# Two transformer blocks on one core: second products of the first weight pair by k, latents' weights in other slots, gate rows and convolutions beside the values

## The chip, the cores and the metric

The kernel runs on 1 core of one Trainium2 chip. A core has a tensor engine (TensorE, PE; PEld is its weight load), a vector engine (VectorE, DVE), a scalar engine (ScalarE, ACT), GpSimd (POOL), the queue engine that issues nearly all DMAs here (SyncE, SP), and 16 DMA engines. Each engine works through its own row of instructions in order and waits on semaphores for the others. The metric is device time in microseconds, median over runs.

## The reference

Two blocks follow one another on 1024 tokens of width 1024, in fp32. The change touches a matrix product of the first block's FFN and the input projection of the second block:

```python
def swiglu(h, w_in, w_out):
    a, b = jnp.split(h @ w_in, 2, axis=-1)
    return (jax.nn.silu(a) * b) @ w_out

# mixer_sublayer of the second block
proj = h @ w_in
(q_m, k_m, v_m, o_m, i_m, f_m, c_q, c_kv, k_r, gate_pre) = jnp.split(proj, IN_SPLIT_POINTS, axis=-1)
qk = jax.nn.silu(causal_depthwise_conv(jnp.concatenate([q_m, k_m], axis=-1), conv_w, conv_b))
log_i = (i_m + igate_b).astype(jnp.float32)
log_f = jax.nn.log_sigmoid((f_m + fgate_b).astype(jnp.float32))
y_m = mlstm_chunkwise(q_m, k_m, v_m, log_i, log_f).reshape(B, S, M_V_WIDTH)
q_a = rms_norm(c_q, q_norm_g) @ w_uq
```

`mlstm_chunkwise` is a recurrence over chunks: inside a chunk a masked product of queries and keys is weighted by exponentials of running sums of `log_f` and `log_i`. The second block then has attention on latents, a merge and a mixture of 32 experts, which the change leaves alone.

## The kernel before

**Products.** Every fp32 operand is cut into a high part (ACT copies it, L163) and a low part (DVE subtracts, L164), and a product is three matmuls: high x high, high x low, low x high (`mm3`, L219 to L221). Weights come by DMA into a `raw` tile and are split into a pair of tiles: `wh`/`wl` from a ring in the weight pool, `uh`/`ul` from the ring `k4`, or a place in a big region (here named `PU`, `SP` or `ML` by what it holds; it is one memory that is reused).

**Order.** A scheduler orders each engine's row from priorities that follow the order in which the code emits; a pool hands out a slot when its last user is done.

**`seven`.** A Strassen-like scheme computes two weight tiles (a pair) times the activations in seven products. It is called twice: in the first block's FFN and in the projection of the second block. The activations of the other half of the tokens come as four sums t1 to t4 and the part "11", made in four steps of k by `block_sums`: 16 PE transposes (L609), four ACT steps (L621, L629 and splits) and nine DVE steps each. The first weight pair is done in the usual way, so that PE has work: `usual_first` for the first half of the tokens, and `usual_second`, called after `block_sums` has ended, for the second half: per weight tile a PSUM tile and 24 matmuls, then an add (L772). Behind them the first Strassen pair starts (L672 on `SP`, whose operands DVE makes by L646 to L653 and splits).

**Projection of the second block**, after `seven(12)`: first the *latents*, eight token tiles of 356 columns (320 for `c_kv` and `k_r`, 36 for the gates, L1006 to L1026), with weights in region `PU`. Per tile ACT reads the PSUM tile, DVE computes a norm in some ten small steps (L105 to L124), ACT writes `ck`, `kr` and `gates` (L1016 to L1020), DVE rotates (L1051 to L1054), PE transposes the gates (L1024) and ACT writes them into the rows LI and FG (L1025, L1026). Then the code emits the eight convolutions (`conv`: a load, four DVE steps L961 and L964, a SiLU on ACT, a store). Then the *values*: two halves `nh` of the columns, eight token tiles each, 24 matmuls of 512 columns per tile; ACT evicts (L1042), SP stores (L1043). The second half's weights lie in `PU`.

**Mixer.** `block2_mixer` begins with `gate_rows` (L1063 to L1100): a chain of DVE and ACT steps on rows of 4 x 1024, which stores two rows to DRAM (`rr`) and transposes LI and FG on PE (L1097, L1098). `mlstm` then runs chunk by chunk between other products (`cq`, L1193): it loads `qkd`, `rr` and `vd` (L1121, L1122, L1127) into the region, now `ML`; POOL makes the decay matrix `Dm` (L1130), ACT its exponentials (L1132), PE the scores (L1135), DVE multiplies (L1137).

Of the kernel before, what the change touches and what calls it, by code (L numbers as in the profile page):

```python
# [11 lines left out]
F32R = mybir.dt.float32r  # L12
I32 = mybir.dt.int32
AF = mybir.ActivationFunctionType
# [6 lines left out]
NT = 8  # L21
# [14 lines left out]
class Kernel:  # L36
# [639 lines left out]
    def seven(self, n, src, B, norms, done, after, beside, kept=None):  # L676
# [4 lines left out]
        nc, V = self.nc, self.nc.vector  # L681
        TH, TL = self.TH, self.TL
        W, TT = {}, {}
# [14 lines left out]
        def first_two(j):  # L698

            A, T = self.left_parts(W[j]), self.T  # L700
            TT[j] = t = {}
            ps = self.pany()
            self.product(ps, A["a11"], T["00"])
            t[0] = self.h2([128, 512], "p1")
            nc.scalar.activation(t[0], ps, AF.Copy)
            yield
            ps = self.pany()
            self.product(ps, A["a12"], T["10"])
            t[2] = self.h2([128, 512], "c11")
            V.tensor_tensor(t[2], ps, t[0], op=OP.add)  # L710
            done(j, 0, 0, t[2], None)
# [37 lines left out]
        parts = [self.left_parts(C[0:2]), self.left_parts(C[2:4])]  # L749
        p1 = []  # L750
# [14 lines left out]
                yield  # L765

        def usual_second():
            for n, (A, p) in enumerate(zip(parts, p1)):
                ps = self.pany()
                self.mm3(ps, [(A[x][0][k], A[x][1][k], self.T[y][0][k], self.T[y][1][k])  # L770
                              for x, y in (("a11", "t1"), ("a12", "11")) for k in range(4)])
                V.tensor_tensor(p, ps, p, op=OP.add)  # L772
                done(0, n, 1, p, p1[0])

        f = usual_first()
        for _ in norms:
            next(f, None)
        for _ in f:
            pass
        f = first_two(1)  # L780
        for _ in self.block_sums(B, kept):
            next(f, None)
        usual_second()
        SP = self.region(1, "SP", F32R)
        for _ in prep(1, True):
            pass
# [182 lines left out]
    def block2_proj(self):  # L969
        nc, tc, a = self.nc, self.tc, self.a  # L970
        dram, const = self.dram, self.const
        W = "w_in_2"
        self.cqd = dram.tile([S, 704], F32, name="cqd")
        self.vd = dram.tile([S, D], F32, name="vd")
        self.gd = dram.tile([16, 128, S], F32, name="gd")
        self.ymd = dram.tile([S, D], F32, name="ymd")

        self.qkr, self.qkd, self.og = [dram.tile([8, 128, S], F32, name=n) for n in ("qkr", "qkd", "og")]
        x01d = dram.tile([4, 128, 512], F32, name="x01d")
        tiles = [(m * 128, self.qkr[m]) for m in range(8)] + [(2048 + m * 128, self.og[m]) for m in range(8)]  # L980
        tiles += [(3784 + m * 128, self.gd[m]) for m in range(8, 16)]

        def done(j, c, half, t, first):
            nc.sync.dma_start(tiles[2 * j + c][1][:, half * 512:half * 512 + 512], t)

        self.seven(12, lambda j: [self.wcols(W, c0, 128) for c0, _ in tiles[2 * j:2 * j + 2]], self.B3, self.norms2, done,
                   lambda: None, lambda j, n: None, x01d)
        for k in range(4):
            t = self.h2([128, 512], "x01")
            nc.sync.dma_start(t, x01d[k])  # L990
            self.split(self.TH[:, k, 512:1024], self.TL[:, k, 512:1024], t)

        cs = self.k4([128, 2, NT, 64], "cs")
        nc.sync.dma_start(cs[:, 0], a["rope_cos"].rearrange("(i p) c -> p i c", p=128))
        nc.sync.dma_start(cs[:, 1], a["rope_sin"].rearrange("(i p) c -> p i c", p=128))
        gb = const.tile([36, 1], F32, name="gbias")
        nc.sync.dma_start(gb[0:4, :], a["igate_b_2"].rearrange("o h -> h o"))
        nc.sync.dma_start(gb[32:36, :], a["fgate_b_2"].rearrange("o h -> h o"))
        self.LI, self.FG = self.k4([4, S], "LI"), self.k4([4, S], "FG")
        PU = self.region(1, "PU", F32R)  # L1000
        units = []
        for u in range(4):
            raw = self.wp.tile([128, 1024], F32, name="raw", bufs=self.raw_bufs)[:, 0:712].rearrange("p (k c) -> p k c", k=2)
            nc.gpsimd.memset(raw[:, :, 324:352], 0.0)
            for c0, n, at in ((3464, 320, 0), (3072, 4, 320), (3076, 4, 352)):
                nc.sync.dma_start(raw[:, :, at:at + n],  # L1006
                                  a[W][0, u * 256:u * 256 + 256, c0:c0 + n].rearrange("(k p) m -> p k m", p=128))
            h, l = [PU[:, 2 * u + n, 0:712].rearrange("p (k c) -> p k c", k=2) for n in range(2)]
            self.split(h, l, raw)
            units += [(h[:, j], l[:, j]) for j in range(2)]  # L1010
        for i in range(NT):
            ps = self.pany((128, 356))
            self.token_rows(ps, i, units)
            ck = self.h2([128, 320], "ck")
            r = self.rstd(self.sumsq(ps[:, 0:256], ck[:, 0:256]), 1, 1.0 / 256)
            nc.scalar.activation(ck[:, 0:256], ps[:, 0:256], AF.Copy, scale=r)  # L1016
            kr = self.h2([128, 2, 64], "kr")
            nc.scalar.activation(kr[:, 0], ps[:, 256:320], AF.Copy)
            gt = self.k2([128, 36], "gates")
            nc.scalar.activation(gt, ps[:, 320:356], AF.Copy)  # L1020
            self.rope(ck[:, 256:320], kr[:, 0], kr[:, 1], cs, i, 1)
            nc.sync.dma_start(self.cqd[i * 128:(i + 1) * 128, 384:704], ck)
            pt, s = self.ptp((36, 128)), slice(i * 128, i * 128 + 128)
            nc.tensor.transpose(pt, gt, self.ident)  # L1024
            nc.scalar.activation(self.LI[:, s], pt[0:4], AF.Identity, bias=gb[0:4])  # L1025
            nc.scalar.activation(self.FG[:, s], pt[32:36], AF.Identity, bias=gb[32:36])  # L1026
        for m in range(8):
            self.conv(m)

        self.yd = dram.tile([S, D], F32, name="yd")  # L1030
        z = self.k4([128, D], "zero")
        nc.gpsimd.memset(z, 0.0)
        for i in range(NT):
            nc.sync.dma_start(self.yd[i * 128:(i + 1) * 128, :], z)

        for nh in range(2):
            units = self.kunits(W, 1024 + nh * 512, 512, 2, 3, PU if nh else None)
            for i in range(NT):
                ps = self.pany()
                self.token_rows(ps, i, units)  # L1040
                t = self.k2([128, 512], "vt")
                nc.scalar.activation(t, ps, AF.Copy)  # L1042
                nc.sync.dma_start(self.vd[i * 128:(i + 1) * 128, nh * 512:nh * 512 + 512], t)  # L1043
# [130 lines left out]

    def block2_mixer(self, dbg=None):
        nc, tc, a = self.nc, self.tc, self.a
        self.gate_rows()
        step = self.mlstm()

        units = []  # L1180
# [822 lines left out]
```

## Time and profile before

| | |
|---|---|
| runs | 2828.6, 2821.66, 2820.65 us; median 2821.66 |
| profiled execution | 2824.64 us |
| its span | 2822.9 us, 36499 instructions |
| mean granted TensorE clock | 0.968 of 2.4 GHz |
| busy share | PE 93%, PEld 75%, DVE 67%, ACT 45%, POOL 8% |

The span runs from the first to the last instruction of the profiled execution; its time is 1.7 us more. Times in the views are microseconds from the span's start. A line in brackets behind a row, as "[6.69 <-DVE SD L1137]", says how long the engine was idle before it and what ended that.

### The profile page before, as it was taken

What the parts mean: (1) busy time and instruction counts of PE and PEld (TensorE: products, weight loads), DVE (VectorE), ACT (ScalarE), POOL (GpSimd) and SP (SyncE); (2) the same over time, 40 slices, a digit from 0 to 9 for tenths busy, and PEclk for the clock granted to TensorE, in tenths of its full rate; (3) what the DMA queues carried; (4) which work ended last, traced back from release to release, by engine and by line L of the source; (5) the groups of instructions that cost most, each with busy time, mean ns of one, the idle gap of its engine ahead of it and who ended that gap; (6) DMA issues with size and microseconds to landing.
All of it is one profiled execution on the core that took longest, in us unless ns stands there. A gap on an engine that the chain in (4) does not pass through costs nothing. (4 is left out here: it accounts for less than half of the span.)

```text
span 2822.9 us, 36499 instructions
## 1 busy us (share of the span) xinstructions
PE 2615.4 (93%) x13018; PEld 2107.2 (75%) x13018; DVE 1884.3 (67%) x3826; ACT 1283.1 (45%) x2258; POOL 221.2 (8%) x207
## 2 busy tenths in 40 slices
PE   6999998999999999889998999999999999889992
PEld 4766676788888787678886788788887887777771
DVE  5666549988887332886558264647778478788885
ACT  4666645333333210342125254425556434677772
POOL 0000002000000000200000000000000200443320
PEclk8999999999999999999999999999999999899996
DMA  7333123455555952533356465650111454799995
GB/s 244 90 98 98 37 75 120 128 165 163 178 172 167 290 181 92 170 106 113 104 159 222 134 184 174 197 194 21 31 31 53 158 196 157 248 335 329 312 319 179
DMA packets 329806, 453.14 MB, mean 161 GB/s; under 512 B 42401, under 2 KB 223710, under 8 KB 329622
## 3 DMA queue, kind: packets, MB, share of 16 engines
q1 hardware_dynamic: 320406, 433.98, 46.8%
q0 software_dynamic: 9216, 16.81, 2.5%
q8 instruction: 103, 1.69, 0.2%
q14 instruction: 81, 0.66, 0.1%
HBM read 360.16 MB, written 107.31 MB: 166 GB/s over the span
## 5 line engine op out<-in xcount | busy, mean ns | idle before, releaser
L163 ACT ACTIVATE wh<-raw 128x1024 fp32r<-128x1024 f32 (+1 forms) x101 | 104.6, 1039 | 185.6 <-DMA raw<-in_ffn_w_in_dram 44.5
L164 DVE TENSOR_TENSOR wl<-raw,wh 128x1024 fp32r<-128x1024 f32 (+1 forms) x101 | 126.0, 1250 | 69.3 <-ACT wh L163 67.1
L551 POOL TENSOR_TENSOR Y<-Y,G 128x1024 f32<-128x1024 f32 x16 | 39.5, 2466 | 1157.1 <-ACT junk L159 1151.9
L164 DVE TENSOR_TENSOR mgl<-X,MH 128x1024 fp32r<-128x1024 f32 x91 | 110.0, 1220 | 12.8 <-ACT MH L163 12.1
L1805 PEld LDWEIGHTS pss<-mgl,xh 128*128 128x128 f32 x512 | 96.9, 189 | 22.6
L252 DVE SCALAR_TENSOR_TENSOR acc<-raw,cc,acc 128x1024 f32<-128x1024 f32 x70 | 89.8, 1282 | 33.9 <-DMA raw<-in_mod_w_dram 31.2
L163 ACT ACTIVATE MH<-X 128x1024 fp32r<-128x1024 f32 x91 | 96.3, 1061 | 32.8 <-DMA X<-in_w_expert_up_dram 13.4
L163 ACT ACTIVATE SP<-raw 128x1024 fp32r<-128x1024 f32 x64 | 67.8, 1060 | 78.7 <-DVE raw L648 43.3
L1803 PE MATMUL pss<-MH,xh 128*128 128x512 f32 x256 | 102.7, 401 | 0.0
L1805 PE MATMUL pss<-mgl,xh 128*128 128x256 f32 x512 | 102.7, 282 | 0.0
L1806 PE MATMUL pss<-MH,xl 128*128 128x512 f32 x256 | 101.3, 396 | 0.0
L442 DVE CUSTOM_DVE_ANT_0 pp<-pss,bias 128x384 f32<-128x384 f32 (+1 forms) x128 | 63.3, 521 | 54.3 <-PE pss L438 53.5
L164 DVE TENSOR_TENSOR SP<-raw,SP 128x1024 fp32r<-128x1024 f32 x64 | 78.0, 1220 | 13.2 <-ACT SP L163 13.2
L219 PE MATMUL pss<-TH,wh 128*128 128x512 f32 x176 | 74.5, 423 | 7.0 <-ACT TH L163 6.9
L228 PE MATMUL mm<-TH,wh 128*128 128x512 f32 x192 | 78.5, 410 | 1.0 <-ACT TH L350 1.0
L449 ACT ACTIVATE pp<-pp,mx 128x384 f32<-128x384 f32 (+1 forms) x128 | 73.8, 579 | 11.6 <-DVE mx L445 11.6
L219 PE MATMUL mm<-WD,mTh 128*128 128x512 f32 x128 | 56.7, 443 | 24.0 <-ACT mTh L163 24.0
L229 PE MATMUL mm<-TL,wh 128*128 128x512 f32 x192 | 77.5, 404 | 0.0
L230 PE MATMUL mm<-TH,wl 128*128 128x512 f32 x192 | 76.7, 399 | 0.0
L220 PE MATMUL pss<-TL,wh 128*128 128x512 f32 x176 | 73.4, 418 | 0.2 <-DVE TL L164 0.2
L221 PE MATMUL pss<-TH,wl 128*128 128x512 f32 x176 | 73.1, 415 | 0.0
L164 DVE TENSOR_TENSOR WD<-X,WD 128x1024 fp32r<-128x1024 f32 x47 | 56.9, 1223 | 21.4 <-ACT WD L163 19.2
(738 smaller groups left out, 8464.9 us busy)
## 6 DMA issues: line engine op xcount, KB each, us to landing
raw<-in_mod_w_dram SPq DMA_DIRECT2D x48, 512.0 KB
X<-in_w_expert_gate_dram SPq DMA_DIRECT2D x47, 512.0 KB
X<-in_w_expert_down_dram SPq DMA_DIRECT2D x47, 512.0 KB
raw<-in_ffn_w_in_dram SPq DMA_DIRECT2D x45, 512.0 KB
X<-in_w_expert_up_dram SPq DMA_DIRECT2D x44, 512.0 KB
raw<-in_w_in_dram SPq DMA_DIRECT2D x41, 512.0 KB
raw<-in_ada_w_dram SPq DMA_DIRECT2D x32, 512.0 KB
midh<-mh SPq DMA_DIRECT2D x44, 256.0 KB
```

The costliest lines, as they stand in the source:

```text
L163: self.nc.scalar.activation(h, src, AF.Copy)
L164: (engine or self.nc.vector).tensor_tensor(l, src, f32(h), op=OP.subtract)
L219: nc.tensor.matmul(ps, ah, bh, start=i == 0, stop=False)
L220: nc.tensor.matmul(ps, ah, bl, start=False, stop=False)
L228: nc.tensor.matmul(ps, ah, bh, start=i == 0, stop=False)
L229: nc.tensor.matmul(ps, ah, bl, start=False, stop=False)
L230: nc.tensor.matmul(ps, al, bh, start=False, stop=i == n - 1)
L252: nc.vector.scalar_tensor_tensor(acc, raw, cc[:, k:k + 1], acc, op0=OP.mult, op1=OP.add)
L449: nc.scalar.activation(P[h][:, :w], P[h][:, :w], AF.Exp, bias=mx[:, h:h + 1], accum_out=den[:, h:h + 1])
L1803: nc.tensor.matmul(ps, xh[:, k], gh, start=k == 0, stop=False)
L1805: nc.tensor.matmul(ps[:, c], xh[:, k], self.ML[n + c][:, m], start=False, stop=False)
L1806: nc.tensor.matmul(ps, xl[:, k], gh, start=False, stop=k == 7)
```

## The change

Four things change; the arithmetic stays. (1) `usual_second` becomes a generator over k that fills both PSUM tiles at once and advances beside `block_sums` from its second step on; the adds (now L778) follow at the end. (2) The latents' weights go to the rings (three units to `wh`/`wl`, one to `uh`/`ul`) in place of the region; of the values' weights the first half now lies in the region and the second in the rings. (3) The gates of all eight tiles are kept in one tile; the eight transposes (L1036) and four evictions of 4 x 512 (L1037, L1038) stand behind the last latents tile. (4) `gate_rows` is called at the second values tile, and one convolution at every odd values tile.

```diff
         def usual_second():
-            for n, (A, p) in enumerate(zip(parts, p1)):
-                ps = self.pany()
-                self.mm3(ps, [(A[x][0][k], A[x][1][k], self.T[y][0][k], self.T[y][1][k])
-                              for x, y in (("a11", "t1"), ("a12", "11")) for k in range(4)])
+            pss = [self.pany(), self.pany()]
+            for k in range(4):
+                for ps, A in zip(pss, parts):
+                    for x, y in (("a11", "t1"), ("a12", "11")):
+                        (ah, al), (bh, bl) = [(m[0][k], m[1][k]) for m in (A[x], self.T[y])]
+                        nc.tensor.matmul(ps, ah, bh, start=(x, k) == ("a11", 0), stop=False)
+                        nc.tensor.matmul(ps, ah, bl, start=False, stop=False)
+                        nc.tensor.matmul(ps, al, bh, start=False, stop=(x, k) == ("a12", 3))
+                yield
+            for n, (ps, p) in enumerate(zip(pss, p1)):
                 V.tensor_tensor(p, ps, p, op=OP.add)
                 done(0, n, 1, p, p1[0])
...
-        f = first_two(1)
-        for _ in self.block_sums(B, kept):
+        f, g = first_two(1), usual_second()
+        for k, _ in enumerate(self.block_sums(B, kept)):
             next(f, None)
-        usual_second()
+            if k:
+                next(g)
+        for _ in g:
+            pass
         SP = self.region(1, "SP", F32R)
...
-        PU = self.region(1, "PU", F32R)
         units = []
...
-            h, l = [PU[:, 2 * u + n, 0:712].rearrange("p (k c) -> p k c", k=2) for n in range(2)]
+            h, l = [t[:, 0:712].rearrange("p (k c) -> p k c", k=2) for t in (
+                [self.wp.tile([128, 1024], F32R, name=n, bufs=self.hl_bufs) for n in ("wh", "wl")] if u < 3 else
+                [self.k4([128, 1024], n, F32R) for n in ("uh", "ul")])]
...
+        gt = self.k4([128, NT, 36], "gates")
...
-            gt = self.k2([128, 36], "gates")
-            nc.scalar.activation(gt, ps[:, 320:356], AF.Copy)
+            nc.scalar.activation(gt[:, i], ps[:, 320:356], AF.Copy)
...
-            pt, s = self.ptp((36, 128)), slice(i * 128, i * 128 + 128)
-            nc.tensor.transpose(pt, gt, self.ident)
+        for half in range(2):
+            pt, s = self.ptp((36, 512)), slice(half * 512, half * 512 + 512)
+            for i in range(4):
+                nc.tensor.transpose(pt[:, i * 128:i * 128 + 128], gt[:, 4 * half + i], self.ident)
             nc.scalar.activation(self.LI[:, s], pt[0:4], AF.Identity, bias=gb[0:4])
             nc.scalar.activation(self.FG[:, s], pt[32:36], AF.Identity, bias=gb[32:36])
-        for m in range(8):
-            self.conv(m)
...
+        PU = self.region(1, "PU", F32R)
         for nh in range(2):
-            units = self.kunits(W, 1024 + nh * 512, 512, 2, 3, PU if nh else None)
+            units = self.kunits(W, 1024 + nh * 512, 512, 2, 3, None if nh else PU)
             for i in range(NT):
+                if nh == 0 and i == 1:
+                    self.gate_rows()
+                if i % 2:
+                    self.conv(4 * nh + i // 2)
...
     def block2_mixer(self, dbg=None):
         nc, tc, a = self.nc, self.tc, self.a
-        self.gate_rows()
         step = self.mlstm()
```

How the rows move on the engines. First, DVE amid the latents, before; L961 and L964 are steps of the convolutions, L113 to L124 of a tile's norm:

```order
L121 SCALAR_TENSOR_TENSOR rs<-ru,rs 128x1
L961 TENSOR_SCALAR co<-cx,cw,cvb 128x1024
L113 SCALAR_TENSOR_TENSOR rt<-rs,ms 128x1
L964 SCALAR_TENSOR_TENSOR co<-cx,cw,co 128x1023
L123 TENSOR_SCALAR rt<-rt 128x1
L964 SCALAR_TENSOR_TENSOR co<-cx,cw,co 128x1021
L124 TENSOR_TENSOR rs<-rs,rt 128x1
L164 TENSOR_TENSOR PU<-raw,PU 128x1024
L964 SCALAR_TENSOR_TENSOR co<-cx,cw,co 128x1022
```

Steps of 1024 columns stand between the steps of one norm there. The row of the changed kernel, also amid the latents:

```order
L105 TENSOR_SCALAR ms<-ss 128x1
L107 TENSOR_SCALAR rs<-ms 128x1
L113 SCALAR_TENSOR_TENSOR rt<-rs,ms 128x1
L119 TENSOR_SCALAR ru<-rt 128x1
L120 TENSOR_TENSOR ru<-ru,rt 128x1
L121 SCALAR_TENSOR_TENSOR rs<-ru,rs 128x1
L113 SCALAR_TENSOR_TENSOR rt<-rs,ms 128x1
L123 TENSOR_SCALAR rt<-rt 128x1
```

The norm's steps now follow one another; in the whole program the convolutions' DVE steps stand behind the last latents tile.

Second, PE at the fourth values tile of the first half, in the changed kernel; LI and FG are the gate rows, transposed by 16 small matmuls:

```order
L221 MATMUL pss<-PU,TL 128x512
L219 MATMUL pss<-PU,TH 128x512
L1112 MATMUL pt<-ident,LI 128x4
L220 MATMUL pss<-PU,TH 128x512
L221 MATMUL pss<-PU,TL 128x512
L219 MATMUL pss<-PU,TH 128x512
```

The first LI transpose has moved in behind the seventh matmul of that tile. Sixteen matmuls further on the other fifteen follow, FG first:

```order
L219 MATMUL pss<-PU,TH 128x512
L220 MATMUL pss<-PU,TH 128x512
L1113 MATMUL pt<-ident,FG 128x4
L1112 MATMUL pt<-ident,LI 128x4
L1113 MATMUL pt<-ident,FG 128x4
```

Before, the same transposes stood behind the last values tile:

```order
L219 MATMUL pss<-PU,TH 128x512
L220 MATMUL pss<-PU,TH 128x512
L221 MATMUL pss<-PU,TL 128x512
L1097 MATMUL pt<-ident,LI 128x4
L1098 MATMUL pt<-ident,FG 128x4
L1097 MATMUL pt<-ident,LI 128x4
```

So their first two wait, within the values, for the results of the gate rows' chain.

Third, DVE at the end of the block sums in the first `seven`, before; L636 is the last sum, `p_4310` and `p_4355` the two tiles of the usual pair, `raw` and `SP` the operands of the first Strassen pair:

```order
L636 SCALAR_TENSOR_TENSOR TL<-pss,B_3702,TH 128x512
L164 TENSOR_TENSOR t4l<-t_4545,t4h 128x512
L164 TENSOR_TENSOR a22l<-raw,a22h 128x512
L646 TENSOR_TENSOR raw<-raw 128x512
L772 TENSOR_TENSOR p_4310<-pss,p_4310 128x512
L648 TENSOR_TENSOR raw<-raw 128x512
L649 TENSOR_TENSOR raw<-raw 128x512
L653 TENSOR_TENSOR raw<-raw 128x512
L164 TENSOR_TENSOR SP<-raw,SP 128x1024
L772 TENSOR_TENSOR p_4355<-mm,p_4355 128x512
L164 TENSOR_TENSOR SP<-raw,SP 128x1024
```

One add of the second products (L772) stood ahead of L648. In the changed kernel:

```order
L636 SCALAR_TENSOR_TENSOR TL<-pss,B_3702,TH 128x512
L164 TENSOR_TENSOR t4l<-t_4571,t4h 128x512
L164 TENSOR_TENSOR a22l<-raw,a22h 128x512
L778 TENSOR_TENSOR p_4310<-pss,p_4310 128x512
L778 TENSOR_TENSOR p_4355<-mm,p_4355 128x512
L646 TENSOR_TENSOR raw<-raw 128x512
L836 TENSOR_TENSOR p_4355<-p_4355,p_4310 128x512
L648 TENSOR_TENSOR raw<-raw 128x512
L649 TENSOR_TENSOR raw<-raw 128x512
L164 TENSOR_TENSOR ml<-p_4355,mh 128x512
L164 TENSOR_TENSOR SP<-raw,SP 128x1024
```

Both adds (L778) and the FFN's product of the two tiles (L836; L827 in the kernel before, where it stands behind the splits) now stand ahead of L648 and of the first split into `SP`.

## Rows read from the trace of the kernel before

**Rows 1.** The page's busy times of the span.
```profile
PE 2615.4 (93%) x13018; PEld 2107.2 (75%) x13018; DVE 1884.3 (67%) x3826; ACT 1283.1 (45%) x2258; POOL 221.2 (8%) x207
```

**Rows 2.** Waits of PE, 1440 to 1665: us in total, times, longest.
```profile
PE pt L1024 <- ACT gates L1020: 10.0, 5, 5.3
PE pt L1135 <- DVE SD L1137: 6.7, 1, 6.7
...
PE mm L220 <- DVE ul L164: 2.2, 1, 2.2
```

**Rows 3.** Table by windows: length, busy PE, PEld, DVE, ACT, POOL, PEclk, DMA, GB/s.
```profile
1490.00:1500.00 10.00, 6.68 (x24) 4.96 (x23) 9.63 (x20) 5.41 (x11) 0.00 (x0) 0.86 0.77 265
1500.00:1510.00 10.00, 4.69 (x16) 3.50 (x15) 10.00 (x21) 2.91 (x9) 0.00 (x0) 0.84 0.81 265
1510.00:1520.00 10.00, 7.84 (x27) 5.59 (x27) 8.95 (x25) 4.74 (x10) 1.54 (x5) 0.84 0.73 289
1520.00:1530.00 10.00, 10.00 (x42) 7.92 (x42) 4.24 (x10) 8.56 (x14) 0.00 (x0) 0.94 0.88 344
1550.00:1590.00 40.00, 40.00 (x184) 32.94 (x182) 2.19 (x2) 6.25 (x10) 0.00 (x0) 1.00 0.23 78
1600.00:1610.00 10.00, 6.52 (x35) 6.52 (x36) 4.19 (x18) 5.10 (x14) 2.78 (x8) 0.68 0.79 175
```

**Rows 4.** Timeline of PE and ACT: first matmuls of three latents tiles, last values eviction.
```profile
1450.63 0.43 PE L219 MATMUL mm<-PU,TH 128*128 128x356 f32 x1 [0.93 <-ACT PU L163]
...
1476.54 0.32 PE L219 MATMUL mm<-PU,TH 128*128 128x356 f32 x1
...
1480.41 0.32 PE L219 MATMUL pss<-PU,TH 128*128 128x356 f32 x1
...
1589.63 0.60 ACT L1042 ACTIVATE vt<-pss 128x512 f32<-128x512 f32 x1 [4.84 <-PE pss L221]
```

**Rows 5.** Groups of DVE by form, 1470 to 1530 (one of L964's three).
```profile
L964 DVE SCALAR_TENSOR_TENSOR co<-cx,cw,co 128x1022 f32<-128x1022 f32 x8 | 10.2, 1280 | 0.0
```

**Rows 6.** Timeline of ACT and DVE: last latents tile, first and last steps of the gate rows.
```profile
1518.07 0.40 ACT L159 ACTIVATE ck<-pss 128x256 f32<-128x256 f32 x1
...
1523.74 1.21 DVE L1063 SCALAR_TENSOR_TENSOR T<-FG 4x1024 f32<-4x1024 f32 x1 [1.79 <-ACT FG L1026]
...
1538.10 1.21 DVE L1077 TENSOR_TENSOR LI<-LI,T 4x1024 f32<-4x1024 f32 x1
...
1543.07 1.06 ACT L1086 ACTIVATE FG<-FG 4x1024 f32<-4x1024 f32 x1 [7.61 <-DVE FG L1085]
```

**Rows 7.** Timeline of POOL and PE at the mixer's first step.
```profile
1600.08 1.26 POOL L1130 TENSOR_TENSOR Dm<-ML,causal 128x512 f32<-128x512 f32 x1 [61.01 <-DMA ML<-rr]
...
1603.48 0.79 PE L1135 MATMUL pt<-ML 128*128 128x128 f32 x2 [6.69 <-DVE SD L1137]
```

**Rows 8.** Waits of PE in the first seven, 470 to 530.
```profile
PE pss L219 <- ACT TH L163: 3.5, 1, 3.5
PE pt L609 <- ACT x L621: 2.4, 1, 2.4
```

**Rows 9.** Table by windows, behind these two waits.
```profile
494.00:497.00 3.00, 3.00 (x9) 2.22 (x8) 3.00 (x6) 0.67 (x2) 0.00 (x0) 0.50 0.00 0
504.25:511.00 6.75, 6.75 (x16) 5.01 (x17) 5.70 (x10) 2.41 (x4) 0.00 (x0) 0.52 0.02 3
```

**Rows 10.** Timeline of DVE, ACT and PE at the end of the block sums.
```profile
507.97 0.68 DVE L164 TENSOR_TENSOR t4l<-t,t4h 128x512 fp32r<-128x512 f32 x1
...
512.55 1.06 ACT L163 ACTIVATE SP<-raw 128x1024 fp32r<-128x1024 f32 x1
...
514.70 0.50 PE L672 MATMUL mm<-TH,SP 128*128 128x512 f32 x1
```

**Rows 11.** Timeline of SP and DVE: a convolution's load and its first use.
```profile
1485.27 1.14 SPq L960 DMA_DIRECT2D cx<-qkr  x1
...
1491.50 0.81 DVE L961 TENSOR_SCALAR co<-cx,cw,cvb 128x1024 f32<-128x1024 f32 x1 [0.37 <-DMA cx<-qkr]
```

## The prediction

> **What bounds the kernel now.** First the page's busy times: TensorE (PE) is busy for 93% of the span [rows 1], so a change is worth what it takes out of PE's idle time or out of the time at the lower clock, and nothing else. Then PE's waits in the two stretches that the change touches. From the latents to the start of the mixer, five waits on the gates (L1020) make 10.0 us, one on a split by VectorE (DVE) 2.2 and the mixer's first step 6.7 [rows 2]; the first weights of the latents cost 0.9 [rows 4]. Then the table by windows, for the clock: 0.84 to 0.94 in the four windows from 1490 to 1530 and 0.68 in that from 1600 to 1610 [rows 3], both behind such waits. DVE is busy for nearly all of 1490 to 1510 [rows 3] while PE waits: the convolutions, three instructions of 1.28 us and one of 0.81 each, eight times over, so 4.65 x 8 = 37 us [rows 5], stand there between the small steps on which a tile's gates depend. Last, the products ahead of the first Strassen pair in the two calls of `seven`: PE waits 2.4 and 3.5 us in the first [rows 8] and runs at the lower clock behind them [rows 9]; the second call shows the same pattern.
>
> **Latents and values.** Bare work, from two starts a tile apart: a latents tile is 3.87 us (1476.54 to 1480.41), a values tile 4.84 + 0.60 = 5.44 between two evictions [rows 4]. So 8 x 3.87 + 16 x 5.44 = 118 us of a stretch that takes 1449.7 (0.93 before the first matmul) to 1589.6 [rows 4], 139.9 us. Of the 22 us between, 10.0 + 2.2 + 0.9 = 13.1 are the waits. The lower level is half speed (1.2 for 2.4 GHz), so a window of 10 us with mean clock c has lost (1 - c) x 10 us if PE had work: 1.4 + 1.6 + 1.6 + 0.6 = 5.2. The rest, about 3.5, are transposes and small steps, and stay.
>
> What goes: latents' weights no longer wait for the region that the products before them hold (0.9). The convolutions are now emitted beside the values, and DVE's new order has all of them behind the last latents tile, so a tile's gates come at the small steps' own pace, and only the last tile's can be late. The eight gate transposes stand at the end, seven of them ahead of the first values tile; ScalarE's (ACT's) order has two weight splits ahead of the seventh tile's gates, which wait until the last tile has read those weights. I put 0.7 us of wait there. The 37 us of DVE work then lie beside 87 us of values on a DVE that is busy for 2.2 of the 40 us from 1550 to 1590 [rows 3]. If that cover were gone they would cost what they do now. ACT switches its function table more often, since the SiLUs now alternate with exponentials; ACT is busy for 6.3 of the same 40 us.
>
> What comes: `gate_rows` is a chain of DVE and ACT steps, 1523.7 to 1539.3 until LI is ready (15.6 us) and to 1544.1 until FG is (20.4) [rows 6]. In the kernel before PE met its results 45 us later, behind all values. Now the order of PE has the first LI transpose seven matmuls into the fourth values tile and the first FG transpose sixteen matmuls later, and PE runs in order. Let E be the end of the latents' matmuls. The chain begins after the last tile's gates: 5.7 us lay between that tile's first reading by ACT and the chain's first step [rows 6], and one weight split stands ahead of it on ACT, so about E + 6.3; LI is there at E + 21.9, FG at E + 26.7. PE comes to the LI transpose at E + 0.7 + 3 x 5.44 + 7 x 0.227 = E + 18.6, with the late gate transpose E + 18.8. It stalls about 3.0 us there. Then 16 matmuls, 3.6 us, and another 1.2 us for FG; or, if the clock falls, the 16 run slower and FG is there. A wait of 2.4 us was followed by 3 us at 0.50, one of 3.5 us by 6.75 us at 0.52 [rows 8, 9]: losses of 1.5 and 3.2 us. I take 5 us for all of it; bounds 0 (the chain runs ahead, since DVE has nothing else) and 10 (the chain 4 us later, and the long clock loss).
>
> Here the sum is 13.1 + 5.2 - 0.7 - 5 = 12.6 us less.
>
> **Start of the mixer.** PE waits 6.7 us, from 1596.8, for the decay matrix of the first step: GpSimd begins it at 1600.1, after 61 us of waiting for a load of gate rows, ACT and DVE follow, and PE goes on at 1603.5 [rows 7]. That load fills a tile which the values' second half of weights occupied until 1589.5. Now those weights lie in the ring of `wh`/`wl`, the region holds the first half's, and is free 43 us earlier; the loads of gate rows and convolved rows stand among the last values stores on the DMA queue (SP). So the 6.7 go, and with them the loss at clock 0.68, (1 - 0.68) x 10 = 3.2 us: 9.9. The 16 small LI and FG transposes only move. What is late next are the mixer's own weights: their slots are those of the values' second half, so their splits wait for the last values tile, and the fourth unit's DMA is issued only after the first split is done. I work it out as landing some 2 us before PE needs it; if it lands 5 us later PE loses 3 and the clock behind that, 5 in all.
>
> **Second products by k.** Nothing is removed: 48 matmuls in each `seven`, in another order. Before, PE waits 3.5 us, then runs them for 6.75 us at clock 0.52 [rows 8, 9], and the first pair starts at 514.70 [rows 10]. Now the parts for k = 0 to 2 fill the gaps while the block sums run. But DVE sets the pace of the sums, to 508.65 [rows 10], and the last k needs its last one; so PE ends at about 509.3. Then DVE's row is: one split, both adds of the second products, and only then the sums for the pair's operands. In the first `seven` a product that waits for ACT stands there too. A step like these is 0.68 us and the next starts 0.6 behind it: from 509.3 the adds to 510.7, L646 to 511.3, L836 to 512.0, L648 to 512.6, then ACT's split of 1.06 [rows 10] to 513.8. Before, one add stood behind that split. So the pair starts at 513.8 for 514.7: 0.9 us gained, 4 us of idle PE in front of it. The second `seven` gives the same by its rows: 0.9. And this gap is the longest now, ahead of work that PE is bound by: 1.5 to 3.2 us of clock, from the two rows above. Sum for each: between -0.9 (the clock stays) and +2.3; I take +1, so 2 us more for both. The page's two waits vanish from those places without a gain: that is what I expect of this part.
>
> The Trainium skill (TensorE: Matmul & The Clock Gate, "HAM oscillation — how this bites in real kernels") says that work in bursts with idle gaps between loses the clock again before each burst, and speaks against this part: filling early gaps only helps if the last one shrinks. The trace agrees, 0.52 behind a gap of 3.5 us [rows 8, 9]; by the rule the sum would be at the +2.3 end for each.
>
> **Sum.** -12.6 - 9.9 + 2 = -20.5 us. The profiled execution took 2824.64 us (span 2822.9 and 1.7 around it), 3.0 above the median of the runs, 2821.66. So 2824.6 - 20.5 = 2804 for one like it, about 2801 for the median. Behind the mixer's start the program is the same and PE stays the bound, so I let the gain stand.
>
> **Rivals.**
> - *The gate chain stalls PE for long.* If ACT's in-order row (evictions of values tiles stand between the chain's steps) puts it 8 us later, PE loses 8 + 3.2 more: 2812. For it: three table loads and nine long steps one after another. Against: before, the same steps with evictions between took the 15.6 us.
> - *The mixer's weights come late*, as above: 5 to 8 us given back, 2806 to 2809. For it: 16 values stores and the loads are on the one queue ahead of that DMA.
> - *More is gained*: the chain runs ahead of PE and the pair's gap costs no clock: 5 + 3.8 better, 2792; with the 3.5 of small steps, 2789.
> - *No change*: both the stall and the weights at their bounds and the pairs at +2.3 each leave -5: within 0.3%, which is 8.5 us and about what a measurement of this kernel can tell from no change.
> - *Slower, by one mechanism*: a convolution is a ring: its load on SP stands behind a values store, that behind an eviction on ACT, that behind the SiLU of the convolution before. One ring must be done in two values tiles, 10.9 us. A load took 6.2 us from issue to use [rows 11]; with 4.65 of DVE and an ACT step of the same width, some 1.06 [rows 10], that is 11.9. If every ring waited for its own load, evictions would come late, and once the buffers are used up PE would wait each time. To lose 20.5 + 8.5 us over seven rounds a ring must take 4.1 us more than two tiles, 15 us. Against: in SP's new order the loads run two or three convolutions ahead.
> - *The change doesn't do what it says*: the latents' first weights still wait, now for ring slots. It costs 0.9.
>
> **How the numbers follow.** My forecast (2795 to 2806) 0.50; long gate stall 0.13; late weights 0.11; more gained 0.14; no change 0.07; slower 0.05. The first four are faster by over 0.3%: 0.88; within it 0.07; slower 0.05. The range from 2786 to 2814 takes in the bounds of all but the last two.
>
> **What would show it.** Right: no waits on gates of over 1 us in the latents; DVE at half load through the values; one PE wait of 2 to 4 us at the LI transpose in the fourth values tile, with the clock down behind it; from the first latents matmul to the last of the values about 127 us for 139.9; the decay matrix long done when PE needs it; in each `seven` one wait of about 4 us ahead of the first pair. Wrong: several waits of PE inside the values (the ring), a wait for `uh` in the mixer's first tile, or a pair that starts 3 us earlier.

## The result, and the profile after

The changed kernel takes 2803.65 us, median of 4 runs (2799.53 to 2805.37), beside 2821.74 for the kernel before in the same runs: a ratio of 0.9929, 95% interval 0.9909 to 0.9948. It is 18 us faster; the forecast was 2801 (2786 to 2814). The profiled execution took 2804.85 us, its span is 2803.1, 19.8 less than before.

The page's line of busy times, which answers to [rows 1]:

```profile
PE 2602.8 (93%) x13018; PEld 2097.4 (75%) x13018; DVE 1886.6 (67%) x3826; ACT 1286.0 (46%) x2250; POOL 223.9 (8%) x207
```

As many matmuls as before, but 12.6 us less of busy PE: no work went away, so this is work that ran at the higher clock (mean granted clock 0.973 for 0.968). The other 7.2 us of the span were idle time.

PE's waits, first those of the first `seven` (470 to 530), then those from the latents to the mixer's start (1440 to 1650):

```profile
PE mm L672 <- ACT SP L163: 4.0, 1, 4.0
PE pss L774 <- DVE TL L636: 2.9, 2, 1.5
...
PE pt L1112 <- DVE T L1094: 2.8, 1, 2.8
PE pss L219 <- ACT cq L1207: 2.1, 1, 2.1
PE mm L220 <- DVE ul L164: 0.6, 1, 0.6
PE pt L1036 <- ACT gates L1030: 0.4, 1, 0.4
```

Against [rows 2]: the five waits on the gates are one of 0.4, the mixer's 6.7 are gone, and one wait has come, 2.8 us for LI (L1112). In the first `seven` the waits of [rows 8] are gone from their places; the first pair (L672) now waits 4.0, and the products by k wait 2.9 us in all for the block sums (L774).

The table by windows, at the first pair and in the values:

```profile
504.25:511.00 6.75, 3.85 (x14) 2.15 (x13) 6.71 (x12) 3.33 (x6) 0.00 (x0) 1.00 0.00 1
511.00:515.00 4.00, 0.77 (x2) 0.67 (x3) 3.97 (x7) 2.08 (x4) 0.00 (x0) 0.76 0.17 66
515.00:520.00 5.00, 5.00 (x14) 3.84 (x13) 2.38 (x3) 1.67 (x2) 0.00 (x0) 0.51 0.53 165
1490.00:1500.00 10.00, 10.00 (x46) 8.27 (x45) 4.24 (x4) 8.74 (x9) 0.00 (x0) 1.00 1.01 393
1500.00:1510.00 10.00, 7.20 (x26) 5.59 (x25) 9.72 (x10) 0.64 (x2) 1.99 (x3) 0.83 0.66 200
1510.00:1520.00 10.00, 10.00 (x55) 8.15 (x54) 9.29 (x10) 5.63 (x6) 0.00 (x0) 1.00 0.32 100
```

DVE is busy for 3.97 of the 4 us in which PE does almost nothing, and the pair then runs at 0.51. In the values only the window with the LI wait is below 1.00; in [rows 3] all four from 1490 to 1530 were.

The timeline: DVE's row ahead of the first pair, and the ends of the stretches.

```profile
508.14 0.75 DVE L636 SCALAR_TENSOR_TENSOR TL<-pss,B,TH 128x512 fp32r<-128x512 f32 x1
...
510.00 0.69 DVE L778 TENSOR_TENSOR p<-pss,p 128x512 f32<-128x512 f32 x1
510.60 0.69 DVE L778 TENSOR_TENSOR p<-mm,p 128x512 f32<-128x512 f32 x1
511.20 0.68 DVE L646 TENSOR_TENSOR raw<-raw 128x512 f32<-128x512 f32 x1
511.80 0.69 DVE L836 TENSOR_TENSOR p<-p,p 128x512 f32<-128x512 f32 x1
512.40 0.69 DVE L648 TENSOR_TENSOR raw<-raw 128x512 f32<-128x512 f32 x1
513.12 1.06 ACT L163 ACTIVATE SP<-raw 128x1024 fp32r<-128x1024 f32 x1
514.23 0.79 PE L672 MATMUL mm<-TH,SP 128*128 128x512 f32 x1 [3.95 <-ACT SP L163]
...
1452.63 0.33 PE L219 MATMUL mm<-wh,TH 128*128 128x356 f32 x1
...
1506.34 0.21 PE L1112 MATMUL pt<-ident,LI 4*128 4x4 f32 x1 [2.80 <-DVE T L1094]
...
1554.62 2.99 POOL L1145 TENSOR_TENSOR Dm<-ML,causal 128x512 f32<-128x512 f32 x2
...
1579.96 0.60 ACT L1057 ACTIVATE vt<-pss 128x512 f32<-128x512 f32 x1 [0.60 <-PE pss L221]
...
1630.70 0.34 PE L221 MATMUL pss<-uh,TL 128*128 128x384 f32 x1
```

Before, the last of these rows, the last matmul of the query latents, was:

```profile
1651.85 0.34 PE L221 MATMUL pss<-uh,TL 128*128 128x384 f32 x1
```

The two adds of the second products (L778) and the FFN's product of the two tiles (L836) stand ahead of the sum L648 that the pair's split needs. GpSimd's part of the decay matrix (L1145) is done some 22 us before PE comes to the scores (L1150), at 1579.71. From the first latents matmul to the last values eviction it is 127.3 us (1452.63 to 1579.96) for 139.0 before (1450.63 to 1589.63), and the first matmul no longer waits 0.9. This stretch is the yardstick of the experiments; they call it the *values stretch*. From the last values eviction to the last query-latents matmul, the *mixer start*, it is 50.7 us for 62.2.

### The profile page after: what moved, and what is told of

It reads as the page before. It is cut to its first block, busy times and chain, and to the rows that moved or that the text cites. A ratio compares the mean times of both kernels' runs of the same rounds, so it can differ in the third digit from the quotient of the medians.

```text
span 2803.1 us, 36494 instructions
## 1 busy us (share of the span) xinstructions
PE 2602.8 (93%) x13018; PEld 2097.4 (75%) x13018; DVE 1886.6 (67%) x3826; ACT 1286.0 (46%) x2250; POOL 223.9 (8%) x207
## 5 line engine op out<-in xcount | busy, mean ns | idle before, releaser
L163 ACT ACTIVATE wh<-raw 128x1024 fp32r<-128x1024 f32 (+3 forms) x104 | 107.1, 1032 | 197.2 <-DMA raw<-in_w_in_dram 47.3
L164 DVE TENSOR_TENSOR wl<-raw,wh 128x1024 fp32r<-128x1024 f32 (+3 forms) x104 | 128.2, 1234 | 77.4 <-ACT wh L163 76.8
L1836 POOL DMA_INDIRECT yd<-ye,tab x32 | 58.4, 1826 | 155.9 <-ACT ye L1835 77.1
L1398 ACT ACTIVATE P<-pss,nm 128x512 f32<-128x512 f32 (+2 forms) x96 | 55.0, 578 | 22.1 <-DVE nm L1394 22.1
L219 PE MATMUL pss<-TH,wh 128*128 128x512 f32 x160 | 64.2, 401 | 0.3 <-DMA lt<-cqd 0.3
```

The lines of the kernel that those rows point to most:

```text
L163: self.nc.scalar.activation(h, src, AF.Copy)
L164: (engine or self.nc.vector).tensor_tensor(l, src, f32(h), op=OP.subtract)
L219: nc.tensor.matmul(ps, ah, bh, start=i == 0, stop=False)
```

## Experiments

All ratios are to the kernel before, run beside it on the same chip; intervals are 95%. Where two experiments are compared with each other, it is by their ratios. 0.1% is 2.8 us.

**1. Second products by tiles alone undone.** The rest is as in the changed kernel.

```diff
-        f, g = first_two(1), usual_second()
+        f = first_two(1)
...
+        usual_second()
```

> The changed kernel with the second products of the usual pair put back as before: by weight tile, behind the block sums, so that PE again has its waits of 2.4 and 3.5 us in each call of seven. Theory (the part by k gains 0.9 us of start and pays a gap of 4 us and the clock behind it): 1.5 to 3 us faster than the changed kernel, about 2801, ratio to before 0.9920 to 0.9925. Rival (the waits that vanish are a gain of the order of their 6 us per call): 5 to 12 us slower than the changed kernel, 2809 to 2816, ratio 0.995 to 0.998.

2800.73 us, 0.9922 (0.9907 to 0.9937). PE's waits in the first `seven` are those of before again, 3.3 and 2.4. By the ratios that is 2 us less than the changed kernel, in the direction of a part that costs, but the intervals overlap: alone this decides nothing.

**2. Second products by tiles of k alone**, in the kernel before.

> The kernel before with the second products by k alone. Theory: PE's waits of 2.4 and 3.5 us go and one of about 4 us ahead of the pair comes, with lower clock behind it; 1 to 3 us slower than before, ratio 1.0004 to 1.001, within what can be told from no change. Rival (a gain): 4 us faster or more, ratio under 0.9985.

2823.15 us, 1.0012 (1.0001 to 1.0022), and the pair waits 3.9 us as in the changed kernel. Slower by some 3 us: with experiment 1, the part costs 2 to 3.

**3. The pair's sums made earlier.** The sums for the first pair's operands advance with the block sums, and the adds of the second products stand behind them on DVE; one small pair of tiles (`a22h`, `a22l`) comes from another ring for it.

```diff
-            yield from self.left_sums(raw, W[j][2:4], W[j][4:])
+            s = []
+            sums = self.left_sums(raw, W[j][2:4], s)
+            for _ in range(2):
+                next(sums)
+                yield
+            s += [SP[:, j % 2 * 4 + n] for n in range(4)]
+            W[j] += s
+            yield from sums
...
-        f, g = first_two(1), usual_second()
+        f, g, q = first_two(1), usual_second(), prep(1, True)
...
             if k:
                 next(g)
-        for _ in g:
-            pass
+                next(q)
+        next(g)
         SP = self.region(1, "SP", F32R)
-        for _ in prep(1, True):
+        for _ in q:
+            pass
+        for _ in g:
             pass
```

> The changed kernel with the sums for the first Strassen pair's operands emitted beside the last block sums (their split of a22 and L646 move ahead of the last step of k) and the adds of the second products behind them. Theory (the gap of 4 us ahead of the pair is DVE's row: both adds and a product stand ahead of L648 and the split): PE's wait ahead of the pair falls from 4.0 and 3.6 us to 1 to 2, the pair starts 2 to 3 us earlier and the clock behind it stays up, 3.5 to 5 us per call, 7 to 10 us faster than the changed kernel, about 2795. Rival (the gap is set by the block sums themselves or by region memory that the split waits for): the same gap, within 2 us of the changed kernel.

2795.09 us, 0.9904 (0.9889 to 0.9918). The pair starts (timeline), and the clock behind it (windows):

```profile
509.47 0.50 PE L672 MATMUL mm<-TH,SP 128*128 128x512 f32 x1 [0.31 <-ACT SP L163]
```
```profile
505.00:510.00 5.00, 4.69 (x12) 2.83 (x11) 4.88 (x9) 2.65 (x5) 0.00 (x0) 0.61 0.00 0
510.00:515.00 5.00, 5.00 (x23) 3.91 (x22) 4.50 (x6) 2.12 (x3) 0.00 (x0) 1.00 0.47 143
```

The wait of 4.0 is 0.3, and from 510 the clock is at its upper level, where the changed kernel stands at 0.51 for 515 to 520. So the gap came from DVE's order, and mending it is worth 0.25%, 7 us, over the two calls.

The lower level has not gone with the gap. In the first call it now lies ahead of the pair (0.61 above), where PE waits for the block sums anyway; in the second it reaches past the pair's start, behind a wait of 0.2:

```profile
1230.00:1233.40 3.40, 2.18 (x5) 1.17 (x4) 3.29 (x6) 1.04 (x1) 0.00 (x0) 0.50 0.00 0
1233.40:1238.00 4.60, 4.53 (x15) 3.65 (x16) 3.89 (x5) 1.08 (x2) 0.00 (x0) 0.72 0.58 173
```
```profile
1233.47 0.79 PE L672 MATMUL mm<-TH,SP 128*128 128x512 f32 x1 [0.21 <-ACT SP L163]
```

Whether filling PE's early gaps pays once the last one is closed is not shown: no run has the early sums with the products by tiles, and the intervals of experiments 1 and 3 overlap.

**4. Gate columns later.** The 16 LI and FG transposes and their copy are emitted at the values' seventh tile; the chain that makes LI and FG stays where the change put it.

```diff
+                if nh == 0 and i == 6:
+                    self.gate_columns()
```

> The changed kernel, but the 16 transposes of LI and FG (and the copy of their result) are emitted at the seventh values tile in place of the second; the gate rows' chain itself starts where it did. Theory (PE's 2.8 us at the first LI transpose and the lower clock behind it are the price of the new place): both go, 4 to 5 us faster than the changed kernel, about 2799, and no PE wait of over 0.5 us in the values. Rival (PE is held there by something else, or the time is given back at the mixer's start, where the same results are needed): within 1 us of the changed kernel.

2795.14 us, 0.9902 (0.9887 to 0.9916). There is no wait at LI; the window with it, in the table by windows:

```profile
1500.00:1510.00 10.00, 10.00 (x46) 8.28 (x45) 9.72 (x10) 0.63 (x2) 2.00 (x3) 1.00 0.60 193
```

The values stretch is 122.8 us (1452.64 to 1575.41), 4.5 less than in the changed kernel: that is what the LI wait costs there with its clock. The mixer start is 1.1 us shorter too (49.6). The ratios give 0.27%, 7.6 us, and the profiled spans 10.1; 4.4 of these 10.1 lie behind the mixer start, where the two programs are the same, so they can't be put down to the wait.

**5. Gate rows in the mixer**, as before the change; all else as in the changed kernel.

```diff
-                if nh == 0 and i == 1:
-                    self.gate_rows()
...
+        self.gate_rows()
         step = self.mlstm()
```

> The changed kernel with gate_rows called at the start of the mixer as before; weights in the new places, gates together, convolutions beside the values. Its chain then still runs early on DVE and ACT, but the LI and FG transposes stand behind the values on PE. Theory (the early call gains nothing by itself and costs PE's wait and clock in the fourth values tile): 3 to 6 us faster than the changed kernel, about 2799, and no wait for the decay matrix at the mixer's start. Rival (the early call is what has the rows stored and loaded in time): PE waits again for the decay matrix, 4 to 8 us slower than the changed kernel.

2797.98 us, 0.9912 (0.9897 to 0.9928). The values stretch is 121.4 us, the shortest of all, and no wait for the decay matrix returns. So the early call takes no wait away, and its transposes cost 3 to 5 us: 5.9 in the stretch, of which 2.5 come back at the mixer start (53.2 us), and 0.17% by the ratios, whose intervals overlap.

**6. Convolutions ahead of the values**, as before the change.

```diff
-                if i % 2:
-                    self.conv(4 * nh + i // 2)
...
+        for m in range(8):
+            self.conv(m)
```

> The changed kernel with the eight convolutions emitted ahead of the values again, as before the change; gates still together, gate rows still in the values, weights in the new places. Theory of the prediction (the place of the convolutions in the code is what took the waits for gates away): the waits come back, 10 us and their clock, 12 to 18 us slower than the changed kernel, 2815 to 2821. Rival (what counts is the row that DVE gets, and that has them behind the latents here too, now between the steps of the gate rows' chain; it is the gathering of the gates that let them slip back): within 4 us of the changed kernel, with no wait for gates of over 1 us, and the LI and FG transposes behind most of the values.

2804.31 us, 0.9937 (0.9925 to 0.9950), the same as the changed kernel. The gate waits do not return (0.5 us). But DVE's row has the convolutions behind the latents all the same. The last latents tile's last step and the first convolution on DVE are:

```profile
1488.22 0.23 DVE L1069 TENSOR_TENSOR ck<-ck,kr 128x64 f32<-128x64 f32 x1
...
1490.74 0.80 DVE L970 TENSOR_SCALAR co<-cx,cw,cvb 128x1024 f32<-128x1024 f32 x1
```

So what fell here is the place in the code as the cause. Whether convolutions between the norm steps make the gates late this run does not test; experiments 8 and 10 do.

**7. Gates transposed tile by tile**, as before the change.

> The changed kernel with the gates transposed tile by tile again (one transpose of 36 x 128 and two evictions of 4 x 128 per latents tile); convolutions and gate rows stay emitted beside the values. In DVE's row the convolutions then stand between the steps of the last two latents tiles' norms, though they are emitted later. Theory after the run with the convolutions ahead (the gathering of the gates is what freed PE from the norm steps): waits for gates of 3 to 8 us come back, 3 to 10 us slower than the changed kernel, 2807 to 2814. Rival (the place of the convolutions in the code decides, both ways are equal): within 2 us.

2801.65 us, 0.9927 (0.9913 to 0.9941); the gate waits are seven short ones, 2.4 us in all. Gathering them does not decide either.

**8. Both of these undone.** What stays of the change are the weights' places, the gate rows and the products by k.

> The changed kernel with both undone that each alone cost little: gates transposed tile by tile and convolutions emitted ahead of the values; weights in the new places, gate rows in the values. In DVE's row the convolutions stand between the norm steps of five of the eight latents tiles. Theory (either of the two is enough to keep the convolutions from the gates, and both together are what takes the 10 us of waits away): the waits for gates come back, 8 to 12 us with lower clock, 10 to 18 us slower than the changed kernel, 2813 to 2820. Rival (the new places of the weights took them away): within 4 us of the changed kernel.

2799.96 us, 0.9927 (0.9912 to 0.9942). With the convolutions ahead and a transpose for each tile, PE's waits are:

```profile
PE pt L1034 <- ACT gates L1030: 2.5, 4, 1.5
PE pt L1110 <- DVE T L1092: 1.1, 1, 1.1
```

2.5 us on gates for 10.0 in [rows 2]. DVE has convolutions between the norm steps of five of the eight latents tiles here. My theory, that this brings 8 to 12 us of waits back, failed, and what is left is mainly the part that I had priced at 0.9: the weights' places.

**9. Places undone.** Latents' weights in the region and the values' second half in it after them, as before; the rest is new.

```diff
-            h, l = [t[:, 0:712].rearrange("p (k c) -> p k c", k=2) for t in (
-                [self.wp.tile([128, 1024], F32R, name=n, bufs=self.hl_bufs) for n in ("wh", "wl")] if u < 3 else
-                [self.k4([128, 1024], n, F32R) for n in ("uh", "ul")])]
+            h, l = [PU[:, 2 * u + n, 0:712].rearrange("p (k c) -> p k c", k=2) for n in range(2)]
...
-            units = self.kunits(W, 1024 + nh * 512, 512, 2, 3, None if nh else PU)
+            units = self.kunits(W, 1024 + nh * 512, 512, 2, 3, PU if nh else None)
```

> The changed kernel with the weights in the places of before: latents' in the region, the values' first half in the rings, the second half in the region; all else new. Theory (the mixer's wait of 6.7 us and its clock came from the region that the values' second half held until the end, not from where the gate rows stand): that wait comes back, with the 0.9 at the latents: 8 to 11 us slower than the changed kernel, 2812 to 2815. Rival (calling the gate rows early is what removed it, since the rows are stored early): within 2 us of the changed kernel.

2814.38 us, 0.9970 (0.9959 to 0.9981). PE's waits:

```profile
PE pt L1148 <- DVE SD L1150: 7.0, 1, 7.0
PE pt L1110 <- DVE T L1092: 3.3, 1, 3.3
...
PE pt L1035 <- ACT gates L1029: 1.9, 2, 1.3
```

The mixer's wait for the decay matrix is back, 7.0 for 6.7. The gate waits are not: 1.9 us. The values stretch is 129.4 us. So with the old places the moved work (convolutions, gathered gates and early gate rows, not tried singly there) does take most of the gate waits away, and with the new places most of them go without it.

**10. Places alone**, in the kernel before: the diff of experiment 9 the other way round.

> The kernel before with the weights' new places alone (latents' in the rings, the values' first half in the region). Theory: the wait of 6.7 us at the mixer's start goes with its clock, the 0.9 at the latents too, and the waits for gates stay: 9 to 12 us faster than before, about 2811, ratio 0.9957 to 0.9968. Rival (the load of gate rows is late for another reason as long as the gate rows are called in the mixer): under 3 us.

2798.31 us, 0.9919 (0.9904 to 0.9935), with convolutions between the norm steps of six of the eight latents tiles (five in the kernel before): the whole gain of the change, about twice the 9 to 12 us of the theory, where the rival gave under 3. I had left something out, and experiment 11 looks for it.

**11. The values' second half alone moved** to the ring, in the kernel before; the latents' weights stay in the region.

```diff
-            units = self.kunits(W, 1024 + nh * 512, 512, 2, 3, PU if nh else None)
+            units = self.kunits(W, 1024 + nh * 512, 512, 2, 3, None)
```

> The kernel before with one thing changed: the second half of the values' weights goes to the rings; latents' weights stay in the region, so that their splits wait for the last pair and hold the load queue. Theory (the loads of the latents and values start some 6 us late because three raw slots wait for the region; all that follows on DVE is late, and so are the gates): the mixer's wait goes (10 us with its clock), waits for gates of 3 us and more with lower clock stay, 8 to 13 us faster than before, about 2810. Rival (the splits of the values' second half, which no longer stand between the last latents tiles' norm steps on DVE, made the gates late): the waits for gates fall below 3 us here too, with the clock at 1.00, and the kernel is 17 to 24 us faster than before, about 2800, as with all the weights in new places.

2810.05 us, 0.9969 (0.9957 to 0.9980). So the second half's place is worth 0.31%, 9 us. The other 0.50%, 14 us, is what experiment 10 has beyond this run: the latents' weights in the rings, and with them the values' first half in the region, where it lies in the rings here. No run has one of these two without the other. Both kernels' rows show how the 14 us come about. With the latents' weights held (this run), the DMA queue, ACT and DVE, then PE's waits and the windows:

```profile
1450.12 1.41 SPq L1006 DMA_DIRECT2D raw<-in_w_in_dram  x3
1452.17 9.72 SPq L189 DMA_DIRECT2D raw<-in_w_in_dram  x6
...
1463.62 0.42 SPq L960 DMA_DIRECT2D cx<-qkr  x1
...
1453.45 0.80 ACT L163 ACTIVATE PU<-raw 128x712 fp32r<-128x712 f32 x1 [2.19 <-DMA raw<-in_w_in_dram]
...
1456.74 0.38 ACT L159 ACTIVATE ck<-mm 128x256 f32<-128x256 f32 x1
...
1457.93 0.15 DVE L105 TENSOR_SCALAR ms<-ss 128x1 f32<-128x1 f32 x1
```
```profile
PE pt L1024 <- ACT gates L1020: 9.2, 5, 6.1
```
```profile
1490.00:1500.00 10.00, 7.21 (x25) 5.11 (x23) 10.00 (x21) 4.04 (x10) 0.00 (x0) 0.83 0.63 229
1500.00:1510.00 10.00, 4.73 (x12) 3.61 (x13) 9.96 (x18) 4.87 (x11) 1.55 (x3) 0.70 0.63 248
```

With both places new (experiment 10), the same views:

```profile
1437.27 1.51 SPq L189 DMA_DIRECT2D raw<-in_w_in_dram  x2
...
1451.12 6.19 SPq L189 DMA_DIRECT2D raw<-in_w_in_dram  x4
...
1459.10 0.35 SPq L960 DMA_DIRECT2D cx<-qkr  x1
...
1452.58 0.39 ACT L159 ACTIVATE ck<-mm 128x256 f32<-128x256 f32 x1
...
1453.35 0.15 DVE L105 TENSOR_SCALAR ms<-ss 128x1 f32<-128x1 f32 x1
```
```profile
PE pt L1025 <- ACT gates L1021: 5.4, 4, 2.6
```
```profile
1490.00:1500.00 10.00, 8.35 (x38) 6.54 (x38) 10.00 (x21) 3.89 (x9) 0.00 (x0) 1.00 0.72 264
1500.00:1510.00 10.00, 10.00 (x45) 8.01 (x44) 10.00 (x21) 4.84 (x10) 0.95 (x1) 1.00 0.54 194
1510.00:1520.00 10.00, 7.43 (x34) 5.85 (x33) 5.87 (x15) 7.15 (x13) 1.26 (x4) 1.00 0.96 379
```

The latents' first matmul is at 1448.89 in the one and 1448.47 in the other, so the times compare as they stand. As long as the latents' weights wait for the region, the raw tiles that they were loaded into stay occupied. The loads behind them need those tiles: the latents' fourth unit (L1006) is loaded only at 1450, and all six loads of the next weights (L189) from 1452, where the other kernel issues two at 1437 and four from 1451; the convolutions' first load goes out 4.5 us later. ACT, whose row is in order, waits for such a load (2.19 us ahead of 1453.45) before it comes to the first tile's sum of squares (L159), 4.2 us later than in the other kernel, and the norm on DVE (L105), on which that tile's gates depend, begins 4.6 us later. The gates then come late by more than PE can cover: 9.2 us of waits for 5.4, and a clock of 0.83 and 0.70 in the first two windows for 1.00. The values stretch is 138.9 us in the one and 127.5 in the other.

**12. Experiments 3 and 4 together.**

> The changed kernel with both mendings: sums for the first pair's operands beside the last block sums, and the LI and FG transposes emitted at the seventh values tile. If the two prices are separate (PE waits at two places that have nothing to do with one another), the gains of 8.5 and 8.5 us add up, at least for 12 of them: 2786 to 2792, ratio to before 0.987 to 0.989. If the second only repeats the first (run-to-run or another bound behind), about 2795.

2785.90 us, 0.9870 (0.9854 to 0.9885): the two gains add, and this is the fastest kernel of the study, 1.3% under the kernel before and 0.6% under the changed one. Its PE waits at the pair and in the values are 0.3 and 0.5 us.

## Why the prediction was right

The time, its sign and nearly every term came out; one attribution did not.

- *Latents and values, -12.6 (127 us).* Measured -12.6: 11.7 of the stretch and 0.9 ahead of it. The two halves hold too. Without the gate rows in it the stretch is 121.4 (experiment 5), 18.5 less than the 139.9 from 1449.7 on, for 13.1 + 5.2 - 0.7 = 17.6; the gate rows give 5.9 back, for 5. The LI wait was forecast at 3.0 us in the fourth values tile and is 2.80; FG costs no wait. DVE is busy for 58.6 of the 90 us from 1490 to 1580, 65%, where half load was forecast.
- *Mixer start, -9.9.* Measured -11.5 (62.2 to 50.7), by the mechanism named: the tile that the values' second half occupied. Experiments 9 and 11 show it from both sides: old place, 7.0 us of wait; that place alone changed, the mixer start is 50.8 us. The next in line, the mixer's own weights, cost 0.6.
- *Second products by k, +2 for both calls.* Measured +2.3: the last add before the latents stands at 1452.83 for 1449.74, 3.1 later, of which 0.8 had come before the first `seven`; alone it costs 3 (experiment 2). Up to the start of the second call it is 1.5, from there 0.8. The first pair starts at 514.23 for a forecast 513.8, behind 3.95 us of idle PE for a forecast 4, and then runs at 0.51 for a time. The rule weighed there (the Trainium skill, TensorE: Matmul & The Clock Gate, "HAM oscillation — how this bites in real kernels") is right in direction, as the trace shows with that 0.51 behind the gap. By it the cost was to be at the upper end, +2.3 for each call, and it is +2.3 for both; and the second call of experiment 3 runs at 0.72 behind a wait of only 0.2.
- *The sum.* These terms make -12.6 - 11.5 + 2.3 = -21.8. With the 0.8 from ahead of the first `seven` and 1.4 behind the mixer start, where the program is the same, that makes -19.6 of the span's -19.8.
- *Rivals.* The long gate stall, late mixer weights, the ring of the convolutions and the change without effect did not occur: in the two stretches no wait is over 4.0 us, and none other in the values is over 0.4.

**The step that failed** is the sentence "latents' weights no longer wait for the region that the products before them hold (0.9)", with the convolutions' move and the gathered gates as what takes the gate waits away. 0.9 is what PE waits. What else was held, the raw tiles, the DMA queue and the splits and norms behind it, I did not follow, though PE's rows have the first matmul waiting for a split into that region [rows 4]. By experiments 10 and 11 the latents' place, together with that of the values' first half, is worth 14 us, 11.4 of them in the values stretch. The total still came out because the two causes are not additive: either alone takes most of the gate waits away (stretch 129.4 with the old places, gate rows included; 127.5 with the new places alone), both together without the gate rows give 121.4. The prediction had one cause at its full price and the other at 0.9, and to that extent the total is luck. The change's other parts add nothing that can be measured to places alone (0.9929 and 0.9919): the moved convolutions and gathered gates save another 6.1 us of the stretch (127.5 to 121.4), and the gate rows and the products by k cost about as much.

Not tried: the latents' weights in the rings with the values' first half left there, which would separate the two places; and new places with the sums of experiment 3 and the gate rows left in the mixer, which could be as fast as experiment 12 with fewer moves.

## What to carry to other kernels

A short wait at the head of a stage can be the visible end of a long one: ask which load tiles the waiting step keeps occupied, what stands behind them on the in-order DMA queue, and which later steps depend on that. Work emitted earlier brings its consumers along: a chain may run early on DVE and ACT while its few matmuls are emitted where their operands are ready (experiment 4). And before filling a bound engine's gaps, read the row of the engine that ends the last gap; there the order of DVE's sums and adds was worth 7 us (experiment 3).

## What the runs showed of the hardware

The length of a wait does not tell by itself whether the clock falls behind it. Waits on the gates of up to 2.6 us, 5.4 in all, left the granted clock at 1.00 in each window of 10 us from 1450 to 1530 (experiment 10); one wait of 2.8 in the changed kernel stands in a window at 0.83, and one of 2.4 in [rows 8, 9] was followed by 0.50. In the second call of experiment 3 the clock stood at 0.50 from 1230 to 1233.4, though no wait of PE in that call, from 1200 on, is over 1.6; PE was busy for 6.7 of the 10 us from 1220 to 1230. Why these differ stays open here; a price per wait taken from one place, as in the prediction, is an estimate.
